# A list scheduler's prices for GpSimd: additions, powers and one-column operations dearer

## The chip, the cores and the metric

The kernel runs on one core of a Trainium2 chip. The metric is the device time of one execution in microseconds. Engines are called as in the profile: PE is TensorE, PEld its weight loads, DVE VectorE, ACT ScalarE, POOL GpSimd, SP SyncE, which issues the transfers.

## The reference, cut to what matters

A decoder trunk of two layers over 1024 tokens of width 1024, everything in float32. Layer 0 mixes by a convolution module, layer 1 by windowed attention on one shared K/V; both have a layer norm behind the mixer, an MLP of width 4096 with a layer norm behind it, and a gated embedding ("ple").

```
for i in range(2):
    if i == 0:
        y = conformer_conv(...)      # w_in, sigmoid gate, 31 taps, layer norm, silu, w_out
    else:
        y = swa_sink_attention(...)  # w_q, rope, window 128, sinks, w_o; K/V from x after layer 0
    x = layer_norm(ALPHA * x + y, mix_g[i], mix_b[i])
    x = layer_norm(ALPHA * x + square(relu(x @ w_up[i])) @ w_down[i], mlp_g[i], mlp_b[i])
    x = x + (p[i] @ w_proj[i]) * sigmoid(x @ w_gate[i])
```

## The kernel before, in words

**The order is planned.** The program does not issue instructions as it goes. `Emit` writes the whole network down as a list of operations (`Recorder.record`), each with its engine, its operands and what it depends on. `Recorder.schedule` then plays that list on a model of the engines and fixes two things for the chip: the order in which each engine takes its instructions, and which buffer of a ring (`SLOTS`: five `t`, sixteen `sm`, six `ps`, two `tr` and so on) a tile gets. In the model an engine takes, of the operations that are ready, the one that was written first; the time after which an operation counts as done is `Recorder.cost`. On the chip the order stays as fixed, but each instruction lasts as long as it lasts, and waits on semaphores for what it needs.

**Operations with a choice.** Additions that are recorded for `either` go in the model to whichever of DVE and GpSimd comes free first. These are the last step of most layer norms (`xt = z * g + b`, the addition) and additions in the embedding stage. `both` and `held` make two-input operations of DVE, and GpSimd's wide ones, exclude each other in the model.

**Precision.** A float32 product is three products of rounded parts: `split` makes a high part `xh` (a rounding copy, "CAST", mostly on ACT) and a low part `xl` (a subtraction on DVE). The same for weights: `raw` arrives by a transfer, ACT makes `wh`, DVE `wl`.

**The places that matter here.** `conv_ln` norms the convolution's output, whose sixteen 128x512 halves lie in the tiles X0 to X7 and A0 to A7. Per 128 tokens: `stats` on DVE, one one-column operation and one power on GpSimd (`sm`, reciprocal root), one one-column operation on DVE (mean times root), then GpSimd scales X and A in place. PE transposes X and A into `tr` or `ps` tiles, ACT applies silu into `t`, and DVE splits `t` into `xh` and `xl`, which frees the `t`. The same `t` ring carries the embedding projections, which ACT copies out of `ps` and SP stores; PE fills its time with those projections while the norm runs. `layer_norm` with `row_stats` closes the mixers and MLPs: three one-column operations and one power on GpSimd per 128 tokens, ACT makes `z`, DVE multiplies, and an `either` adds into `x` (tiles E and B in layer 0, A and B in layer 1). `to_xT` then transposes `x` on PE and splits it.

Of the kernel before, what the change touches and what calls it, by code (L numbers as in the profile page):

```python
# [13 lines left out]
ALU = mybir.AluOpType  # L14
# [185 lines left out]
class Recorder:  # L200
# [90 lines left out]
    def cost(self, o, outs, allv):  # L291
        e, n = o.eng, o.name
        f = outs[0].n if outs and isinstance(outs[0], View) else 1024
        if e == "tensor":
            if n == "transpose":
                return 113.5
            return max(109.0, f * 0.4427 + 5.5 * (f < HT))
        if e == "sync":
            return 380.0
        if e == "scalar":  # L300
            t = 60.0 + f * 0.85
            if n == "activation":
                t += sum(c for k, c in (("bias", 90.0), ("scale", 130.0), ("accum_out", 110.0)) if isinstance(o.kw.get(k), View))
            return t
        if e == "gpsimd":
            if n == "tensor_tensor":
                return 460.0 if o.kw["op"] == ALU.pow else 90.0 + 2.2 * f
            return 160.0 + 1.17 * f
        psum = any(v.buf.space == "PSUM" for v in allv)
        if n == "tensor_scalar" and not psum:  # L310
            return 100.0 + f * 0.69
        if n == "bn_stats":
            return 69.0 + 1.042 * allv[-1].n
        if n == "reduce_max":
            return 70.0 + allv[-1].n * 1.042
        if n == "reciprocal":
            return 60.0 + 6.3 * f
        t = 120.0 if isinstance(o.kw.get("scalar"), View) else 70.0
        return t + f * 1.042
# [1676 lines left out]
```

## Time and profile before

| | |
|---|---|
| median of 3 runs | 2141.74 us (2140.77 to 2145.2) |
| profiled execution, whole | 2140.78 us |
| its span, first to last instruction | 2139.1 us |
| PE busy | 2118.0 us, 99% |
| DVE busy | 1736.6 us, 81% |
| ACT busy | 1144.6 us, 54% |
| GpSimd busy | 285.7 us, 13%, 530 instructions |

PE has work at nearly every moment, so the time is what PE must do and the few microseconds in which it stands still. A table of waits names, for each engine, what ended its idle time. In a timeline a bracket at the end of a row gives the idle time ahead of it and what ended that. All work is recorded through one helper, so all rows carry L469 and are told apart by their tiles.

### The profile page before, as it was taken

Reading aid. Unit: us, or ns where it says so; the run is one execution under the profiler, and the core shown is the slowest. Engines: PE = TensorE matmul, PEld = TensorE weight load, DVE = VectorE, ACT = ScalarE, POOL = GpSimd, SP = SyncE. Lnnn points to the kernel's source line nnn. Section 1 sums busy time; section 2 is a strip of 40 time slices with the busy share of each in tenths; the row PEclk is TensorE's granted clock in tenths of the full one; section 3 lists DMA queues with packets and bytes.
Section 4 is the critical chain, followed back from the end, with each engine's and each line's share of the span. In section 5 each row is a group of like instructions: output and inputs, shape, how many; then the busy total and the mean of one; then the engine's idle time right before and its main releaser. Section 6 shows DMA issues by size and latency. Waiting matters only on the chain.

```text
span 2139.1 us, 29650 instructions
## 1 busy us (share of the span) xinstructions
PE 2118.0 (99%) x9940; PEld 1748.0 (82%) x9940; DVE 1736.6 (81%) x2823; ACT 1144.6 (54%) x2162; POOL 285.7 (13%) x530
## 2 busy tenths in 40 slices
PE   9999999999999999999999999999999999999999
PEld 7888778888888888888788878888888888888877
DVE  6566678898898888876986888689988988788688
ACT  5455673554544633335755888455445554333484
POOL 0000042300000000001310666250000000000042
PEclk9999999999999999999999999999999999999999
DMA  8654664747787856655487022665778785565726
GB/s 256 174 151 142 198 217 159 249 151 257 268 278 266 302 175 208 204 180 211 161 281 252 14 87 80 214 229 190 258 262 294 263 332 173 180 233 170 263 72 233
DMA packets 209928, 443.16 MB, mean 207 GB/s; under 512 B 21744, under 2 KB 57200, under 8 KB 209776
## 3 DMA queue, kind: packets, MB, share of 16 engines
q1 hardware_dynamic: 209776, 441.27, 62.2%
q8 instruction: 78, 1.28, 0.2%
q14 instruction: 74, 0.61, 0.1%
HBM read 296.75 MB, written 144.44 MB: 206 GB/s over the span
## 4 chain that ended last, share of the span: by engine, by line
PE 45%; ACT 2%; DVE 2%; DMA 2%; issue 1%; POOL 0%; SPq 0%; DVEq 0%; ACTq 0%; POOLq 0%
PE ps L469 31%; PE tr L469 14%; ACT z L469 1%; DMA raw<-in_w_kv_dram 0%; ACT wh L469 0%; ACT xh L469 0%; DVE t L469 0%; DMA raw<-form 0%; POOL sm L469 0%; DMA raw<-gate_t 0%; DVE B L469 0%; ACT t L469 0%; DVE z L469 0%; DMA raw<-in_w_q_dram 0%; DMA B<-xsp 0%
## 5 line engine op out<-in xcount | busy, mean ns | idle before, releaser
L469 PE MATMUL ps<-xh 128*128 128x512 f32 x618 | 240.4, 389 | 0.0
L469 PE MATMUL ps<-xl,xh 128*128 128x512 f32 x618 | 240.4, 389 | 0.0
L469 PE MATMUL ps<-xh,xl 128*128 128x512 f32 x618 | 240.4, 389 | 0.0
L469 ACT CAST wh<-raw 128x1024 fp32r<-128x1024 f32 (+2 forms) x158 | 148.2, 941 | 154.9 <-PE ps L469 90.5
L469 PE MATMUL ps<-xl,wh 128*128 128x512 f32 x540 | 210.9, 391 | 0.3 <-DVE xl L469 0.3
L469 PE MATMUL ps<-xh,wl 128*128 128x512 f32 x540 | 210.6, 390 | 0.0
L469 PE MATMUL ps<-xh,wh 128*128 128x512 f32 x540 | 209.3, 392 | 0.4 <-ACT xh L469 0.4
L469 POOL TENSOR_SCALAR sm<-sm 128x1 f32<-128x1 f32 x72 | 25.8, 362 | 1363.7 <-DVE E L469 600.8
L469 PE MATMUL ps<-wh,xh 128*128 128x512 f32 x392 | 154.6, 395 | 2.5 <-DVE t L469 1.5
L469 PE MATMUL ps<-wl,xh 128*128 128x512 f32 x392 | 155.0, 395 | 0.0
L469 PE MATMUL ps<-wh,xl 128*128 128x512 f32 x392 | 154.7, 395 | 0.0
L469 ACT CAST xh<-wh 128x1024 fp32r<-128x1024 f32 x76 | 79.9, 1051 | 116.5 <-PE ps L469 90.3
L469 ACT CAST wh<-g 128x512 fp32r<-128x512 f32 x108 | 65.1, 621 | 140.0 <-DVE g L469 56.2
L469 PEld LDWEIGHTS ps<-xh,xl 128*128 128x128 f32 x618 | 116.0, 188 | 24.3
L469 PEld LDWEIGHTS ps<-xh 128*128 128x128 f32 x618 | 116.0, 188 | 24.0
L469 PEld LDWEIGHTS ps<-xl,xh 128*128 128x128 f32 x618 | 116.0, 188 | 23.9
L469 DVE TENSOR_TENSOR wl<-raw,wh 128x1024 fp32r<-128x1024 f32 (+1 forms) x102 | 103.9, 1020 | 36.1 <-ACT wh L469 34.8
L469 PEld LDWEIGHTS ps<-xh,wh 128*128 128x128 f32 x540 | 101.7, 188 | 22.1 <-ACT xh L469 0.8
L469 PEld LDWEIGHTS ps<-xl,wh 128*128 128x128 f32 x540 | 101.6, 188 | 20.7 <-DVE xl L469 1.4
L469 PEld LDWEIGHTS ps<-xh,wl 128*128 128x128 f32 x540 | 101.4, 188 | 20.6
L469 DVE TENSOR_TENSOR xl<-wh,xh 128x1024 fp32r<-128x1024 f32 x76 | 93.0, 1223 | 24.3 <-ACT xh L469 24.3
L469 DVE TENSOR_TENSOR E<-z,cst 128x832 fp32r<-128x832 f32 x64 | 64.0, 1021 | 57.9 <-PE ps L469 57.9
(425 smaller groups left out, 5642.1 us busy)
## 6 DMA issues: line engine op xcount, KB each, us to landing
wh<-hid SPq DMA_DIRECT2D x78, 512.0 KB, 4.4
raw<-in_w_up_dram SPq DMA_DIRECT2D x61, 512.0 KB, 4.3
wl<-in_w_down_dram SPq DMA_DIRECT2D x58, 512.0 KB, 4.7
hid<-zz SPq DMA_DIRECT2D x96, 256.0 KB, 3.4
hid<-t SPq DMA_DIRECT2D x70, 256.0 KB, 3.0
raw<-hid SPq DMA_DIRECT2D x30, 512.0 KB, 3.8
scr<-zz SPq DMA_DIRECT2D x32, 256.0 KB, 3.7
B<-scr SPq DMA_DIRECT2D x64, 128.0 KB, 4.0
```

The lines of the kernel that those rows point to most:

```text
L469: getattr(getattr(nc, o.eng), o.name)(*a, **k)
```

## The change

Three prices of GpSimd in the model are raised. `f` is the number of columns.

```diff
         if e == "gpsimd":
             if n == "tensor_tensor":
-                return 460.0 if o.kw["op"] == ALU.pow else 90.0 + 2.2 * f
-            return 160.0 + 1.17 * f
+                return 550.0 if o.kw["op"] == ALU.pow else 90.0 + 3.1 * f
+            return (300.0 if n == "tensor_scalar" and f < 8 else 160.0) + 1.17 * f
```

For the shapes that occur: an addition of 512 columns goes from 1216 to 1677 ns, a power from 460 to 550 ns, a one-column operation from 161 to 301 ns. Scalings of 512 columns keep their price of 759 ns. No instruction computes anything else than before. The order on PE is the same up to the convolution's layer norm and differs in places from there on: in the layer norms, the embedding stage of layer 0, the K/V stage and the attention. In the long MLP stages PE's order is the same but for tile numbers. Ten `either` additions move from DVE to GpSimd and nine from GpSimd to DVE.

The first place is the convolution's layer norm. GpSimd before, from the scaling of the tokens of X5 on; `sm12` and `sm6` are the roots for the tokens of X6 and X7:

```order
L469 TENSOR_SCALAR X5_351_619<-X5_351_619,sm13_650_2915 128x512
L469 TENSOR_SCALAR A5_19_83<-A5_19_83,sm13_650_2915 128x512
L469 TENSOR_SCALAR sm12_655_2939<-sm10_652_2928 128x1
L469 TENSOR_SCALAR sm6_659_2957<-sm3_657_2944 128x1
L469 TENSOR_TENSOR sm12_655_2939<-sm12_655_2939,mhalf_242_306 128x1
L469 TENSOR_TENSOR sm6_659_2957<-sm6_659_2957,mhalf_242_306 128x1
L469 TENSOR_SCALAR X6_352_630<-X6_352_630,sm12_655_2939 128x512
```

GpSimd now, at the same place:

```order
L469 TENSOR_TENSOR sm13_650_2915<-sm13_650_2915,mhalf_242_306 128x1
L469 TENSOR_TENSOR sm12_655_2939<-sm12_655_2939,mhalf_242_306 128x1
L469 TENSOR_SCALAR X5_351_619<-X5_351_619,sm13_650_2915 128x512
L469 TENSOR_SCALAR A5_19_83<-A5_19_83,sm13_650_2915 128x512
L469 TENSOR_SCALAR X6_352_630<-X6_352_630,sm12_655_2939 128x512
L469 TENSOR_SCALAR A6_20_84<-A6_20_84,sm12_655_2939 128x512
L469 TENSOR_SCALAR sm6_659_2958<-sm3_658_2947 128x1
L469 TENSOR_TENSOR sm6_659_2958<-sm6_659_2958,mhalf_242_306 128x1
```

The power for `sm12` has moved ahead of X5 and A5, and the one for `sm6` behind X6 and A6. DVE beside it, before (the one-column products with `sm12` and `sm6` stand ahead of the split of the first `t`):

```order
L469 TENSOR_TENSOR wl4_671_3003<-raw1_644_2878,wh3_670_3002 128x1024
L469 SCALAR_TENSOR_TENSOR sm12_655_2939<-sm10_652_2928,sm12_655_2939 128x1
L469 SCALAR_TENSOR_TENSOR sm6_659_2957<-sm3_657_2944,sm6_659_2957 128x1
L469 CAST xh00_243_307<-t1_679_3027 128x2x256
L469 TENSOR_TENSOR xl00_244_308<-t1_679_3027,xh00_243_307 128x2x256
L469 TENSOR_TENSOR wl3_672_3005<-raw0_675_3010,wh4_673_3006 128x1024
L469 TENSOR_TENSOR xl00_244_308<-t2_682_3038,xh00_243_307 128x2x256
```

DVE now:

```order
L469 SCALAR_TENSOR_TENSOR sm12_655_2939<-sm10_652_2928,sm12_655_2939 128x1
L469 TENSOR_TENSOR wl3_671_3002<-raw0_673_3006,wh4_672_3003 128x1024
L469 CAST xh00_243_307<-t1_679_3028 128x2x256
L469 TENSOR_TENSOR xl00_244_308<-t1_679_3028,xh00_243_307 128x2x256
L469 SCALAR_TENSOR_TENSOR sm6_659_2958<-sm3_658_2947,sm6_659_2958 128x1
L469 TENSOR_TENSOR xl00_244_308<-t2_681_3037,xh00_243_307 128x2x256
```

The product with `sm6` now stands between the split of tile t1 and that of tile t2. On ACT, the copies of the projections out of `ps` were, before, the next thing after the first silu half of t4:

```order
L469 CAST xh00_243_307<-t2_682_3038 128x2x256
L469 ACTIVATE t4_690_3077<-tr0_695_3107,cst_240_304 128x256
L469 COPY t1_700_3125<-ps0_680_3030 128x512
L469 ACTIVATE t4_690_3077<-tr0_695_3107,cst_240_304 128x256
L469 COPY t0_693_3088<-ps4_677_3020 128x512
```

ACT now:

```order
L469 ACTIVATE t4_689_3074<-tr0_697_3113,cst_240_304 128x256
L469 ACTIVATE t2_704_3139<-ps1_698_3115,cst_240_304 128x256
L469 ACTIVATE t4_689_3074<-tr0_697_3113,cst_240_304 128x256
L469 ACTIVATE t2_704_3139<-ps1_698_3115,cst_240_304 128x256
L469 CAST xh10_247_311<-t4_689_3074 128x2x256
L469 COPY t0_691_3084<-ps4_676_3018 128x512
L469 COPY t1_701_3131<-ps0_680_3031 128x512
```

The silu into the slot t2, which the split of the old t2 frees, now stands ahead of both copies.

The second place is PE in the last layer norm of the first MLP. Before, the transposes of the tile B3 (the normed tokens 512 to 639) stand here; the products around them are those of the embedding's gate:

```order
L469 MATMUL ps2_1607_9254<-wh0_1538_8811,xh00_243_307 128x512
L469 MATMUL ps2_1607_9254<-wl0_1546_8877,xh00_243_307 128x512
L469 MATMUL ps3_1612_9281<-ident_241_305,B3_961_4546 128x128 x4
L469 MATMUL ps2_1607_9254<-wh0_1538_8811,xl00_244_308 128x512
L469 MATMUL tr1_1615_9298<-wh3_1548_8896,xh10_247_311 128x512
```

Now they stand here:

```order
L469 MATMUL ps2_1615_9317<-wh1_1529_8714,xh00_243_307 128x512
L469 MATMUL ps2_1615_9317<-wl0_1544_8864,xh00_243_307 128x512
L469 MATMUL ps2_1615_9317<-wh1_1529_8714,xl00_244_308 128x512
L469 MATMUL ps4_1613_9301<-ident_241_305,B3_958_4534 128x128 x4
L469 MATMUL ps5_1616_9324<-ident_241_305,B5_1348_6974 128x128 x4
L469 MATMUL ps2_1615_9317<-wh0_1538_8811,xh00_243_307 128x512
```

That is 19 products later than before, counted over PE's whole order. Other transposes move likewise, named by their start in the trace of before: those at 1022.95 us by 11 rows, at 1035.96 us by 10, at 1095.87 us by 8, at 1138.36 us by 10. The product that started at 1045.40 us stands 8 rows earlier. On DVE, the addition that frees the `ps` of the product of 2070.83 us stands 11 rows earlier.

## The prediction

> **What bounds the kernel now.** I read the busy times first, then what each stretch leaves PE idle, then PE's waits.
>
> ```profile
> PE 2118.0 (99%) x9940; PEld 1748.0 (82%) x9940; DVE 1736.6 (81%) x2823; ACT 1144.6 (54%) x2162; POOL 285.7 (13%) x530
> ...
> 250.00:300.00 50.00, 46.23 (x248) 39.17 (x249) 31.34 (x64) 36.60 (x74) 24.52 (x32) 0.97 0.86 274
> 400.00:450.00 50.00, 49.63 (x223) 40.19 (x222) 48.09 (x77) 28.66 (x48) 2.86 (x2) 1.00 0.56 177
> 500.00:1000.00 500.00, 500.00 (x2207) 413.33 (x2206) 418.70 (x586) 228.02 (x333) 0.00 (x0) 1.00 0.72 242
> 1000.00:1050.00 50.00, 47.99 (x240) 38.79 (x239) 42.13 (x77) 40.34 (x79) 23.03 (x37) 1.00 0.15 50
> 1050.00:1100.00 50.00, 49.13 (x228) 40.17 (x227) 45.35 (x71) 32.26 (x52) 10.72 (x3) 1.00 0.79 278
> ```
>
> The first row is the page's; the others are windows (length, then busy time and count of PE, PEld, DVE, ACT, POOL, then PE's clock). PE stands still for 2139.1 - 2118.0 = 21 us of the whole span. From 500 to 1000 us it is never idle, and 500 us over 2207 products gives 0.227 us for each, which I use as the price of a row of PE. There the order can't matter. It can matter where a window has less than its 50 us: 3.8 us missing about the convolution's norm, 2.0 and 0.9 us about the last norm of the first MLP.
>
> ```profile
> PE ps L469 <- ACT t L469: 4.0, 2, 2.7
> PE ps L469 <- DVE t L469: 3.9, 5, 1.5
> PE ps L469 <- DMA B<-scr: 2.6, 2, 1.9
> ...
> PE ps L469 <- ACT zz L469: 0.9, 1, 0.9
> PE ps L469 <- POOL B L469: 0.8, 2, 0.4
> ```
>
> PE's waits (sum, times, longest): the largest, 2.7 us, is one wait for ACT's copies into `t`. GpSimd itself is named with 0.8 us only. It acts through others.
>
> **The prices themselves.** The groups of GpSimd (busy, mean ns | idle):
>
> ```profile
> L469 POOL TENSOR_TENSOR B<-z,g 128x512 f32<-128x512 f32 x16 | 26.1, 1645 | 10.4 <-DVE z L469 7.0 <-PE tr L469 1.7 <-DVE sm L469 1.0
> L469 POOL TENSOR_SCALAR sm<-sm 128x1 f32<-128x1 f32 x72 | 25.8, 362 | 1363.7 <-DVE E L469 600.8 <-DVE A L469 589.0 <-DVE sm L469 156.0
> L469 POOL TENSOR_TENSOR sm<-sm,mhalf 128x1 f32<-128x1 f32 x40 | 24.2, 610 | 2.9
> L469 POOL TENSOR_TENSOR A<-A,t 128x512 f32<-128x512 f32 x3 | 12.3, 4111 | 25.0 <-DVE t L469 19.9 <-PE ps L469 5.1
> L469 POOL TENSOR_TENSOR B<-B,bo 128x512 f32<-128x512 f32 x1 | 1.3, 1297 | 16.6 <-issue 16.6
> ...
> 1064.82 8.84 POOL L469 TENSOR_TENSOR E<-E,t 128x512 f32<-128x512 f32 x1 [18.93 <-DVE t L469]
> ```
>
> The new prices (1677, 550 and 301 ns) are nearer to the means of 1645, 610 and 362 than the old (1216, 460, 161). But the same addition lasts 1.30 us alone and up to 8.84 us beside DVE, so a fixed price is a plan, not a time. No work goes away. What the change is worth is what the new order does to PE's 21 us.
>
> [...]
>
> **Term 1, the convolution's norm.** Timelines of POOL, DVE, ACT and PE:
>
> ```profile
> 280.44 0.78 POOL L469 TENSOR_SCALAR A<-A,sm 128x512 f32<-128x512 f32 x1
> 282.91 1.83 POOL L469 TENSOR_SCALAR X<-X,sm 128x512 f32<-128x512 f32 x1
> 287.10 0.47 POOL L469 TENSOR_SCALAR sm<-sm 128x1 f32<-128x1 f32 x2
> 287.65 1.06 POOL L469 TENSOR_TENSOR sm<-sm,mhalf 128x1 f32<-128x1 f32 x2
> 288.71 1.01 POOL L469 TENSOR_SCALAR X<-X,sm 128x512 f32<-128x512 f32 x1
> ...
> 283.03 1.23 DVE L469 TENSOR_TENSOR wl<-raw,wh 128x1024 fp32r<-128x1024 f32 x1
> 288.75 0.16 DVE L469 SCALAR_TENSOR_TENSOR sm<-sm,sm 128x1 f32<-128x1 f32 x1 [0.36 <-POOL sm L469]
> 289.27 0.98 DVE L469 TENSOR_TENSOR xl<-t,xh 128x512 fp32r<-128x512 f32 x1
> 291.31 0.68 DVE L469 TENSOR_TENSOR xl<-t,xh 128x512 fp32r<-128x512 f32 x1
> ...
> 290.29 0.59 ACT L469 COPY t<-ps 128x512 f32<-128x512 f32 x1 [2.36 <-DVE xl L469]
> 290.77 0.57 ACT L469 ACTIVATE t<-tr,cst 128x256 f32<-128x256 f32 x1
> ...
> 287.16 0.60 PE L469 MATMUL ps<-ident,X 128*128 128x128 f32 x4
> 287.60 0.60 PE L469 MATMUL tr<-ident,X 128*128 128x128 f32 x4
> 290.93 0.50 PE L469 MATMUL ps<-wh,wh 128*128 128x512 f32 x1 [2.73 <-ACT t L469]
> ```
>
> The chain reads backwards: PE waits at 290.93 for ACT's copy of 290.29, which needs a free `t`, which DVE's `xl` of 289.27 frees, which stood behind the product with `sm6` (288.75), which waited for GpSimd's power (done at 287.65 + 1.06 = 288.71).
>
> Now that power stands behind X6 and A6, and the splitting of t2, not t1, is what ACT needs first. GpSimd, from the end of the scaling of A3 (281.22): one one-column operation more ahead, 0.24, and the power for `sm8`, 0.53: 281.99. Two one-column operations, 0.47, X4 and A4, 0.78 each, plus 1.05 for the `wl` that DVE runs beside them (1.83 against 0.78): 285.07. Two powers: 286.13. X5, A5, 1.56, beside the moved `wl` 1.05: 288.74. X6 beside the CAST, 1.01, A6 beside an `xl`, 0.78 + 0.98: 291.5. One-column, 0.24, power, 0.53: 292.3, against 288.71. Then DVE's product, 0.16, and `xl`, 0.68: 293.1. ACT runs four silu halves and casts, about 0.45 apart (0.48 from 290.29 to 290.77), and the copy, 0.59, so that PE goes on at about 295.7, where it was 290.93. It does two groups of transposes more meanwhile, 2 x 0.44 (from 287.16 to 287.60). **+4.8 - 0.9 = +3.9 at most**. Without any collision on GpSimd (0.78 for every scaling) the power ends near 289.1 and the same steps give 292.5 - 290.93 - 0.9 = **+0.7 at least**. A gain would need the power to come earlier, and two more scalings stand ahead of it. I take **+3.4**, near the upper end, since both `wl` rows stand beside those scalings in DVE's order too.
>
> **Term 2, waits that go.** PE's rows with the waits that a later place can hide:
>
> ```profile
> 1022.95 0.63 PE L469 MATMUL ps<-ident,E 128*128 128x128 f32 x4 [0.49 <-DVE E L469]
> 1029.39 0.65 PE L469 MATMUL ps<-ident,B 128*128 128x128 f32 x4 [0.32 <-POOL B L469]
> 1035.96 0.66 PE L469 MATMUL ps<-ident,B 128*128 128x128 f32 x4 [0.43 <-POOL B L469]
> 1045.40 0.50 PE L469 MATMUL ps<-wh,xh 128*128 128x512 f32 x1 [0.76 <-DVE t L469]
> 1095.87 0.66 PE L469 MATMUL ps<-ident,B 128*128 128x128 f32 x4 [0.62 <-DVE xl L469]
> 1138.36 0.41 PE L469 MATMUL ps<-ident,t 128*128 128x128 f32 x2 [0.54 <-DVE B L469]
> 2070.83 0.50 PE L469 MATMUL ps<-wh,xh 128*128 128x512 f32 x1 [0.71 <-DVE t L469]
> ```
>
> The transposes of 1022.95, 1029.39, 1035.96, 1095.87 and 1138.36 move 11, 19, 10, 8 and 10 rows back, at least 1.8 us each, against waits of 0.3 to 0.6: they go, 0.49 + 0.32 + 0.43 + 0.62 + 0.54 = 2.4. The wait at 2070.83 goes too, since the addition that frees its `ps` stands 11 rows earlier on DVE: 0.7. Together **-3.1**; as the same waits can come back at a neighbour, between 0 and -3.1. What is late next: the splits behind those transposes, which the products of the next stage need.
>
> **Term 3, a wait that grows.** The product of 1045.40 comes 8 rows earlier, 1.8 us, for an addition on DVE that keeps its place: between 0 and 1.8 more. DVE's own work ahead of it also depends on PE, so I take half, **+0.9**.
>
> **Term 4, the nineteen additions.** Those that go to GpSimd cost DVE 0.7 us less each, those that come 0.7 to 1.7 more; the balance is one. In the first mixer's norm three come to DVE where it is busy 48.09 of 50 us; two of them late would cost up to 2 us, one early gives nothing. **+0.5**, 0 to 2. The rest lies beside PE's products.
>
> **Term 5, the attention and the other norms.** PE's transposes shift both ways there by up to 19 rows. I take **0**, with -1.5 to +2.
>
> Sum: 3.4 - 3.1 + 0.9 + 0.5 = **+1.7 us**. On the profiled execution, 2140.8 (1.7 around its span), that is 2142.5. The median of the runs, 2141.7, lies 0.9 above it, so the forecast is **2143.4**. The least sum is 0.7 - 3.1 - 1.5 = -3.9, the largest 3.9 + 1.8 + 2 + 2 = 9.7.
>
> **Rivals.** 0.2% is 4.3 us, about what a measurement of this kernel can tell from none.
>
> *Faster.* Later transposes and the truer prices take away most waits everywhere, the one at 290.93 too, because `xl` of t1 comes ahead of `sm6` now and may let PE on. For it: every wait listed is short. Against it: the copies stand behind the silu into t2. It decides if ACT's copy starts before 289.5; then term 1 is -1.5 instead of +3.4, and with terms 3 and 4 at 0 and 5 at -1.5 the sum is -6.1: 2135.6.
>
> *Slower.* One addition on GpSimd beside back-to-back work of DVE holds up a tile that PE transposes for K/V. Four of the ten that move to GpSimd lie between 1060 and 1145 us, where DVE is busy 45.35 of 50 and one addition took 8.84 us. Planned at 1.68, it ends 7.2 late; PE can run some 11 rows, 2.5 us, ahead: +4.7, 2148.1. It decides once an addition there lasts over 4.2 us and its tile is the next one wanted. Against it: the long one of before made PE wait for nothing in that list.
>
> *Nothing.* Waits only change places, and the 2.7 us stays about what it is: 2141.7.
>
> **How the numbers follow.** Forecast 0.43 (of it 0.03 above the upper bound of no change, 2146.0), nothing 0.09, slower 0.28, faster 0.20 (0.01 more from the forecast's lower edge, 2137.5). So slower 0.31, faster 0.21, same 0.48. Alone, the likeliest case spans 2139 to 2147. For 8 in 10 the range takes in the nearer halves of both rivals: 2136 to 2149.
>
> **What would show it.** The window 250 to 300 with PE at 43 instead of 46.23, and one wait of 6 to 7 us for ACT's `t` near 295; the waits on POOL B and DVE E gone; a wait of 1 to 2.5 us on DVE `t` near 1044; GpSimd additions of over 4 us between 1060 and 1145. I am wrong if PE goes on before 293 in the first place, or if the attention between 1150 and 1350 gains or loses over 2 us.

## The result and the profile after

The changed kernel takes 2155.44 us (median of 4 runs, 2152.2 to 2157.16); the kernel before 2142.3 us (4 runs, 2140.77 to 2145.2). The ratio is 1.0062 (95% interval 1.0050 to 1.0074): slower by about 13 us. The forecast was 2143.4 us with a range up to 2149, so the time lies outside it, on the side of the slower rival. The profiled execution is the longest of the four runs (2157.16 us) and the one of before the shortest of its runs (2140.78), so the two traces differ by 16.4 us, 3 us more than the medians.

First the page of the changed kernel, its span and busy times, then windows (length, busy time and count of PE, PEld, DVE, ACT, POOL, PE's granted clock, DMA share, GB/s):

```profile
span 2155.4 us, 29646 instructions
...
PE 2123.4 (99%) x9940; PEld 1750.9 (81%) x9940; DVE 1733.4 (80%) x2822; ACT 1146.4 (53%) x2162; POOL 277.7 (13%) x531
...
250.00:300.00 50.00, 44.45 (x233) 37.18 (x234) 29.70 (x62) 35.00 (x71) 22.32 (x32) 0.93 0.80 264
...
1000.00:1050.00 50.00, 49.39 (x245) 40.70 (x245) 40.44 (x72) 37.35 (x74) 21.21 (x36) 1.00 0.14 41
...
1150.00:1200.00 50.00, 47.28 (x242) 39.07 (x241) 33.42 (x99) 33.79 (x103) 11.59 (x32) 0.97 0.56 193
```

PE now stands still for 2155.4 - 2123.4 = 32.0 us instead of 21, and has 5.4 us more busy time with the same 9940 products: part of them ran at a lower clock (0.93 against 0.97 in the window 250 to 300, 0.97 against 1.00 from 1150 to 1200). The window 250 to 300 lost 1.8 us of PE's work (44.45 against 46.23), 1000 to 1050 gained 1.4, and 1150 to 1200, where PE was busy for 49.52 us before, lacks 2.7.

PE's waits in the changed kernel (sum in us, times, longest):

```profile
PE tr L469 <- ACT t L469: 5.5, 4, 3.2
PE ps L469 <- DVE xl L469: 3.0, 2, 2.2
...
PE ps L469 <- DMA wl<-gate_low_t: 2.2, 1, 2.2
```

The waits on POOL `B` and DVE `E` of before are gone, as the prediction said. Waits of over 2 us are four now, 3.2, 2.5, 2.2 and 2.2, where before had one.

To see where the time went, take the two traces and the start of the same row of PE by count (row 1376, row 1700 and so on). PE has the same number of rows in both, so the time between two such rows can be compared though the order within differs (only at row 5420 do five of the rows ahead of it differ too):

| PE's stage | before, us | after, us | difference |
|---|---|---|---|
| up to the convolution's norm | 272.4 | 270.5 | -1.9 |
| convolution's norm | 69.3 | 74.2 | +4.9 |
| first mixer's output and norm | 130.8 | 132.2 | +1.4 |
| first MLP | 535.3 | 536.1 | +0.8 |
| last norm of the first MLP | 43.5 | 41.8 | -1.7 |
| embedding of layer 0 | 50.8 | 52.5 | +1.7 |
| K/V, entry into the attention | 67.3 | 70.5 | +3.2 |
| attention, second mixer | 371.7 | 373.1 | +1.4 |
| second MLP and its norm | 546.4 | 546.9 | +0.5 |
| end | 45.6 | 51.5 | +5.9 |

The order on PE ahead of the convolution's norm is the same in both; the -1.9 there is a stretch of half clock at 252 us that the trace of before has and this one hasn't (0.50 against 1.00 from 252 to 255). Two things follow for the reading. Times of the two traces can't be set side by side as they stand: the changed kernel reaches row 1376, the start of the convolution's norm, at 272.05 us, the kernel before at 273.95, so 1.9 us have to be added to a time of the changed kernel near 290 to put it on the clock of before. And each line of the table is one execution of each kernel; how far the same order can differ from one execution to the next is told in the last section.

**The convolution's norm.** POOL, DVE, ACT and PE in the changed kernel, then two windows:

```profile
284.80 1.99 POOL L469 TENSOR_SCALAR A<-A,sm 128x512 f32<-128x512 f32 x1
...
289.07 0.55 POOL L469 TENSOR_TENSOR sm<-sm,mhalf 128x1 f32<-128x1 f32 x1
...
289.65 0.16 DVE L469 SCALAR_TENSOR_TENSOR sm<-sm,sm 128x1 f32<-128x1 f32 x1 [2.33 <-POOL sm L469]
289.73 0.69 DVE L469 TENSOR_TENSOR xl<-t,xh 128x512 fp32r<-128x512 f32 x1
...
290.51 0.56 ACT L469 ACTIVATE t<-ps,cst 128x256 f32<-128x256 f32 x1 [2.40 <-DVE xl L469]
...
285.82 0.66 PE L469 MATMUL tr<-ident,A 128*128 128x128 f32 x4 [0.90 <-ACT t L469]
287.71 0.66 PE L469 MATMUL tr<-ident,X 128*128 128x128 f32 x4 [0.76 <-ACT t L469]
291.58 1.11 PE L469 MATMUL tr<-ident,A 128*128 128x128 f32 x4 [3.22 <-ACT t L469]
...
290.00:297.00 7.00, 5.42 (x18) 4.59 (x19) 5.12 (x9) 5.79 (x12) 2.49 (x2) 0.52 0.32 98
```

The chain is the forecast one: PE waits for ACT's silu, ACT for a free `t2`, that for DVE's split of 289.73, which stands behind the product with `sm6`, which waits for GpSimd's power. The power ends at 289.07 + 0.55 = 289.62, on the clock of before 291.5, which is 2.8 us later than its 288.71. The kernel z_conv below, which has the same order here and starts the stage within 0.13 us of before, says the same without a correction, 291.15 + 0.55 = 291.70:

```profile
291.15 0.55 POOL L473 TENSOR_TENSOR sm<-sm,mhalf 128x1 f32<-128x1 f32 x1
```

There are three waits in the changed kernel, each ahead of a group of transposes, 0.90 + 0.76 + 3.22 = 4.9 us, instead of the one of 2.73: 2.2 more. Behind them PE is granted half its clock for about 7 us: 5.42 us of work at 0.52 could have been done in 2.8, another 2.6 lost. 2.2 + 2.6 = 4.8, against 4.9 in the table.

**The end.** One row of PE's waits, POOL and SP before:

```profile
PE tr L469 <- DMA wl<-gate_low_t: 0.3, 1, 0.3
...
2097.12 9.44 POOL L469 TENSOR_TENSOR A<-A,t 128x512 f32<-128x512 f32 x1 [19.15 <-DVE t L469]
...
2106.59 0.34 SPq L469 DMA_DIRECT2D out_dram<-A  x1
2107.97 0.32 SPq L469 DMA_DIRECT2D wl<-gate_low_t  x1
```

and in the changed kernel, with one row of DVE, PE and windows:

```profile
2109.12 11.85 POOL L469 TENSOR_TENSOR A<-A,t 128x512 f32<-128x512 f32 x1 [24.14 <-DVE t L469]
...
2119.71 0.70 DVE L469 TENSOR_TENSOR zz<-zz,tr 128x512 f32<-128x512 f32 x1
...
2120.99 0.34 SPq L469 DMA_DIRECT2D out_dram<-A  x1
2121.39 0.42 SPq L469 DMA_DIRECT2D wl<-gate_low_t  x1
...
2122.35 0.47 PE L469 MATMUL ps<-wh,xh 128*128 128x512 f32 x1 [1.30 <-DVE zz L469]
2126.40 0.80 PE L469 MATMUL ps<-wl,xh 128*128 128x512 f32 x1 [2.20 <-DMA wl<-gate_low_t]
...
2095.00:2125.00 30.00, 27.48 (x118) 21.51 (x116) 30.00 (x51) 18.36 (x28) 12.71 (x2) 1.00 0.53 181
2126.00:2130.00 4.00, 3.60 (x9) 2.88 (x10) 0.38 (x1) 0.59 (x1) 1.55 (x2) 0.57 1.02 384
```

One addition on GpSimd, beside a DVE that is never idle (30.00 of 30 us), takes 11.85 us, where its new price is 1.68. It ends 1.26 us after the start of DVE's row at 2119.71, the first in that time that takes one of its inputs from a `tr` or `ps` tile; the last section comes back to this. The store of its tile waits for it on SP, and the load of the weight `wl` stands behind that store; PE then waits 2.20 us for `wl`. Before, the same addition took 9.44 us and the same store stood ahead of the same load, but PE waited only 0.3 us for it. Counted from row 9730, where the end begins, the addition was over after 17.6 us then and is after 21.5 now, and the load went out after 19.0 and 21.9. So the store's place is not new; before, the addition was simply over in time. After the waits PE is again at about half clock (0.57): 3.60 us of work there cost some 1.5 more than at full clock.

**The entry into the attention.** PE and a window in the changed kernel:

```profile
1165.60 0.47 PE L469 MATMUL ps<-wh,xh 128*128 128x512 f32 x1 [2.46 <-ACT B L469]
...
1167.00:1170.00 3.00, 3.00 (x8) 2.19 (x8) 1.97 (x9) 1.56 (x4) 0.00 (x0) 0.51 0.92 300
```

A product waits 2.46 us, and half clock follows here too: 3 us of work at 0.51, and with 1170 to 1171, which has 0.75, some 3.4 us at half clock in all. The longest wait of that stretch before:

```profile
1162.48 0.41 PE L469 MATMUL ps<-ident,t 128*128 128x128 f32 x2 [0.47 <-ACT X L469]
```

### The profile page after: what moved, and what is told of

Same layout as the page of the kernel before. It is cut to its first block, busy times and chain, and to the rows that moved or that the text cites. A ratio compares the mean times of both kernels' runs of the same rounds, so it can differ in the third digit from the quotient of the medians.

```text
span 2155.4 us, 29646 instructions
## 1 busy us (share of the span) xinstructions
PE 2123.4 (99%) x9940; PEld 1750.9 (81%) x9940; DVE 1733.4 (80%) x2822; ACT 1146.4 (53%) x2162; POOL 277.7 (13%) x531
## 3 DMA queue, kind: packets, MB, share of 16 engines
q8 instruction: 78, 1.28, 0.2%
## 4 chain that ended last, share of the span: by engine, by line
PE 77%; DVE 4%; ACT 3%; DMA 2%; POOL 1%; issue 1%; SPq 0%; DVEq 0%; ACTq 0%; POOLq 0%
PE ps L469 58%; PE tr L469 19%; ACT z L469 1%; DVE xl L469 1%; POOL A L469 1%; DMA raw<-gate_t 1%; ACT wh L469 1%; DMA t<-proj 1%; ACT t L469 1%; DVE z L469 0%; DVE sm L469 0%; DVE X L469 0%; DMA xh<-in_w_gate_dram 0%; ACT xh L469 0%; DVE t L469 0%
## 5 line engine op out<-in xcount | busy, mean ns | idle before, releaser
L469 PE MATMUL ps<-xh 128*128 128x512 f32 x636 | 247.4, 389 | 0.0
L469 PE MATMUL ps<-xl,wh 128*128 128x512 f32 x584 | 228.1, 391 | 0.0
L469 PE MATMUL ps<-xh,wl 128*128 128x512 f32 x584 | 227.3, 390 | 0.0
L469 PE MATMUL ps<-xh,wh 128*128 128x512 f32 x584 | 226.2, 391 | 0.4 <-ACT xh L469 0.4
L469 PE MATMUL ps<-wh,xh 128*128 128x512 f32 (+1 forms) x388 | 155.0, 400 | 7.6 <-ACT B L469 2.5
L469 PE MATMUL ps<-wl,xh 128*128 128x512 f32 (+1 forms) x388 | 154.9, 399 | 2.2 <-DMA wl<-gate_low_t 2.2
L469 PE MATMUL ps<-wh,xl 128*128 128x512 f32 (+1 forms) x388 | 154.4, 398 | 0.0
L469 PEld LDWEIGHTS ps<-xh,wh 128*128 128x128 f32 x584 | 109.9, 188 | 24.7 <-ACT xh L469 0.8
L469 PEld LDWEIGHTS ps<-xh,wl 128*128 128x128 f32 x584 | 109.7, 188 | 22.4
L469 PEld LDWEIGHTS ps<-xl,wh 128*128 128x128 f32 x584 | 109.9, 188 | 21.3 <-DVE xl L469 0.6
```

Of the source, the lines that this page charges most:

```text
L469: getattr(getattr(nc, o.eng), o.name)(*a, **k)
```

## Experiments: which place loses how much

The schedule is one greedy pass, so a price that holds only for the operations of one stage (they are numbered in program order) gives the changed order there and leaves the old one nearly everywhere else.

```diff
         if e == "gpsimd":
+            if o.num < 3200:                 # z_conv
+            if 3200 <= o.num < 5000:         # z_mix0, instead
+            if 5000 <= o.num < 13500:        # z_mid, instead
+            if 18000 <= o.num:               # z_end, instead
+                ...the three new prices...
             if n == "tensor_tensor":
                 return 460.0 if o.kw["op"] == ALU.pow else 90.0 + 2.2 * f
             return 160.0 + 1.17 * f
```

> The new prices hold only for the operations up to the convolution's layer norm; the order there is the changed kernel's, row by row, and from the first MLP on the old kernel's. Theory A (each place loses by itself what its own waits and its own slow clock show): +4.4 us on the old kernel, 2146 to 2147, PE's three waits for ACT's t near 286, 288 and 291 us of 0.9, 0.8 and 3.2 us, and some 6 us at a granted clock of 0.5 behind 290. Theory B (the loss is a matter of the whole, as of drifting transfers, and one place alone loses little): within 1.5 us of the old kernel.

> The new prices hold only for the operations of the first mixer's output and its layer norm. Theory A: the waits of 1.5 us for DVE's wl at 400 and 0.7 and 0.2 us for ACT's t behind it come back, +2.1 us, and perhaps +0.8 at 612: 2144 to 2145. Theory B: within 1 us of the old kernel.

> The new prices hold only from the last layer norm of the first MLP through the embedding stage, K/V and the attention. Theory A: -1.7 us in the norm, +1.4 in the embedding, +3.8 at the entry into the attention (a wait of 2.5 us for ACT near 1158 and 3.4 us of half clock behind it): +3.5, 2145 to 2146. Theory B: within 1.5 us of the old kernel.

> The new prices hold only from the last layer norm of the second MLP to the end. Theory A: GpSimd's last long addition again takes about 12 us, PE again waits 1.3 us for DVE's zz and 2.2 us for the load of wl near 2110, with 3.4 us of half clock behind: +5.5, 2147 to 2148. Theory B: within 1.5 us of the old kernel.

The kernel before took 2140.92 us beside these four. z_conv: 2145.55, ratio 1.0022 (1.0013 to 1.0031). z_mix0: 2144.59, 1.0021 (1.0012 to 1.0030). z_mid: 2144.27, 1.0016 (1.0007 to 1.0025). z_end: 2147.15, 1.0030 (1.0019 to 1.0042). Each part alone is slower; together they make 0.89%, more than the whole's 0.62% (0.50 to 0.74). They share one reference, so their errors add up together and the sum is loose. The second mixer's norm, in which three of the nineteen additions change engine, is in none of the four.

In its own trace z_mix0 loses only 1.1 us in its own stage. Most of the rest, 3.8 us in the first MLP, is a wait near 610 us, in a stage whose order on PE is that of before, and half clock behind it:

```profile
610.02 0.74 PE L473 MATMUL tr<-X,wh 128*128 128x512 f32 x2 [1.97 <-ACT t L473]
...
604.00:620.00 16.00, 14.03 (x55) 11.09 (x54) 12.22 (x21) 5.63 (x11) 0.00 (x0) 0.89 0.76 261
```

That wait is 0 in before and in z_conv, 0.62 in the changed kernel, 1.39 in z_mid, with the same rows around it: it comes and goes. What it follows from was not found, so z_mix0's time, in the range of theory A, is in part luck.

## Experiments: the convolution's norm

> The kernel with the new prices for the convolution's norm alone (z_conv), and in it one row moved by hand: DVE's split of t2 stands ahead of the product with sm6, which waits for GpSimd's power. Theory A (that one product, queued in front of the split, holds ACT and so PE): ACT's wait of 2.4 us for DVE's xl goes, PE's wait of 3.2 us near 291 falls under 1.2, the clock stays at 1.0 there; 2145.5 falls to 2141 to 2142. Rival (GpSimd's late scalings of X5 to X7 hold PE's next transposes in any case): the wait only changes its name and the time stays within 1 us of z_conv.

```diff
-            for o in self.schedule():
+            order = self.schedule()          # prices as in z_conv
+            ahead(2805, 3029)                # DVE: split xl of t2 ahead of the product with sm6
+            for o in order:
```

2142.27 us against 2141.75, ratio 1.0002 (0.9993 to 1.0011): the loss of z_conv is gone from the time, by one row of DVE. PE and a window in it:

```profile
288.91 0.66 PE L492 MATMUL tr<-ident,A 128*128 128x128 f32 x4 [0.89 <-ACT t L492]
290.36 0.50 PE L492 MATMUL ps<-wh,wh 128*128 128x512 f32 x1 [0.34 <-ACT t L492]
...
290.00:296.00 6.00, 4.89 (x25) 3.85 (x25) 5.27 (x9) 5.00 (x10) 2.83 (x2) 1.00 0.46 154
```

The last wait is 0.89 + 0.34 us instead of 3.26 in z_conv, and without a long wait the clock stays at 1.00 in this trace. The shorter waits ahead of it are still there, and a new one of 0.77 us for GpSimd's scaling of A, so the rival is right in a small part: all of PE's waiting in this stage falls from 4.9 to 3.5 us only. The stage takes 71.0 us against z_conv's 74.2, and more than half of the 3.2 between them is the half clock that no longer follows. GpSimd's power is no earlier than in z_conv (it ends at 289.96, and this trace is 2.2 us ahead of z_conv's); what counted was that a split which needs nothing from it stood behind it in DVE's queue.

The same holds in the kernel before, whose 2.73 us wait has this cause too. There the splits of both tiles were moved ahead of the products with `sm12` and `sm6`, with the old prices:

```diff
+            # DVE: cast and split of t1, split of t2, ahead of the product with sm12
+            order = self.merge(self.schedule(), ((2794, 3018), (2795, 3018), (2805, 3018)))
```

> The kernel before, with its own order but for three rows of DVE in the convolution's norm: the rounding of t1 and the splits of t1 and t2 stand ahead of the two products with sm12 and sm6 that wait for GpSimd. Theory A: the wait of 2.7 us, PE's longest, shrinks to under 1 us: 2138 to 2139.5, faster than both kernels. Rival (X6 and X7 are scaled later instead and PE waits for them): within 1 us of the kernel before.

2139.53 us against 2141.75, ratio 0.9990 (0.9981 to 0.9999): a little faster than the kernel before, just clear of the noise. The wait falls to

```profile
289.85 0.50 PE L516 MATMUL ps<-wh,wh 128*128 128x512 f32 x1 [0.79 <-ACT t L516]
```

## Experiments: the end

> The kernel with the new prices for the end alone (z_end), and in it SP's store of the tile that GpSimd adds to for 12 us moved behind the three loads of weights that stood behind it. Theory A (the store waits for the addition and holds the loads in SP's queue): the load of wl is issued some 2 us earlier, PE's wait of 2.2 us for it goes and the 3 to 6 us of half clock behind it with it; 2147.2 falls to 2142.5 to 2144, leaving the waits near 2075 and 2111. Rival (the buffer of wl comes free late, or the transfers themselves are slow): within 1 us of z_end.

```diff
+            behind(19573, 19750)             # SP: store of A behind the three loads; prices as in z_end
```

2143.03 us against 2141.75, ratio 1.0008 (0.9999 to 1.0017), where z_end had 1.0030.

```profile
2097.28 11.85 POOL L492 TENSOR_TENSOR A<-A,t 128x512 f32<-128x512 f32 x1 [24.00 <-DVE t L492]
...
2107.65 0.32 SPq L492 DMA_DIRECT2D wl<-gate_low_t  x1
2109.87 0.42 SPq L492 DMA_DIRECT2D out_dram<-A  x1
```

The addition is as long as in z_end, and PE no longer waits for `wl`, for which it waited 2.72 us there, with a granted clock of 0.66 over the 10 us from 2114 on: the late addition cost time through the store that stands ahead of the loads in SP's queue, not by its length alone.

> As z_end, with the long addition itself done by DVE instead of GpSimd, at its place in the order. Theory A: 0.7 us on DVE instead of 12 on GpSimd, the store and the loads behind it go out early: 2142.5 to 2144.5, some 0.5 more than with the store moved, since DVE has no idle time there. Rival (DVE is what bounds this stretch): as z_end or up to 1 us more.

```diff
+            ops[19572].eng = "vector"        # the long addition on DVE; prices as in z_end
```

2144.74 us, ratio 1.0013 (1.0005 to 1.0022). Taking the long addition away from GpSimd also recovers more than half. Where the rest lies its trace does not settle: PE waits 1.18 us for ACT's `wh` at the end, but that stage is 1.0 us shorter than in s_end_sp, and the stage ahead of it is 1.1 us longer, since here half clock follows a wait of 2.19 us that both kernels have there (the products behind it start 0.43 us apart, in s_end_sp 0.23). The two repairs can't be told apart by their times.

## Experiments: the entry into the attention

Three tries, each on top of the one before it, with the prices of z_mid.

> As z_mid (new prices from the last norm of the first MLP through the attention), with five rows of the K/V stage moved by hand: ACT's two copies of the third tile of keys and values stand ahead of a weight's rounding, and DVE's three products that release that tile's ps stand ahead of the K splits, as in the kernel before. Theory A (the queues of ACT and DVE hold the last reader of the ps that PE wants): PE's wait of 2.5 us at the entry into the attention and the 3.4 us of half clock behind it go; +3.4 on the kernel before falls to 0 or below, 2140.5 to 2142, since the norm ahead of it is 1.7 us shorter. Rival (transfers of w_q are late there): as z_mid.

> The middle part's new order (operations 5000 to 13499) with six rows restored: the five of the run before (ACT's two copies of one K/V tile ahead of a weight rounding, DVE's three zz additions of that tile ahead of the first K addition) and, new, DVE's addition t<-zz of the same tile ahead of the two K additions too. Theory, the transposes waited 2.11 us for t because that addition stood behind two K additions and the split of X on DVE, which in turn waited for ACT's K copies: it can now run near 1154.9 instead of 1157.77, PE's wait at the transposes goes, and the stretch at the entry of the attention falls from 22.4 us to 19.6 to 20.5; the time to 1.0002 of the kernel before (0.9993 to 1.0010), from 1.0014. Rival, the wait moves on again, to the next tile's transposes or to the products behind them: the stretch stays at 22 us and the ratio at 1.0010 to 1.0018.

> The middle part's new order with thirteen rows of the attention's entry restored: the six of the run before, three DVE rows of the last K/V tile (zz, zz, t) ahead of the split of X, and on PE the two pairs of transposes of the last two K/V tiles, each four products later, as in the kernel before. Theory, the entry loses because PE's new order asks for these transposes two and eight products behind the ones before them, where it was six and ten, while the chain ACT's copies, DVE's zz additions, t for one tile takes as long as before; each repair on one engine alone therefore only moved the wait. With both, PE's wait of 2.42 us goes: the entry takes 19.6 to 20.4 us, not 22.6, and the time is 1.0000 to 1.0006 of the kernel before. Rival, another wait takes its place again (the products behind the transposes, for a ps): the entry stays over 21.5 us, the ratio at 1.0010 to 1.0016.

```diff
+            # s_att, one K/V tile. ACT: two copies ahead of a rounding; DVE: three zz additions
+            # ahead of the first K addition
+            (10497, 10555), (10500, 10555), (10501, 10471), (10502, 10471), (10503, 10471)
+            # s_att2, further. DVE: t<-zz of that tile ahead of the first K addition
+            (10504, 10471)
+            # s_att3, further. DVE: zz, zz, t of the last tile; PE: two pairs of transposes
+            # four products later
+            (10521, 10132), (10522, 10132), (10523, 10132)
+            (10506, 10588), (10507, 10588), (10525, 10598), (10526, 10598)
```

| kernel | ratio to before (95%) | entry (rows 5330 to 5420), us |
|---|---|---|
| before | | 19.6 |
| z_mid | 1.0016 (1.0007 to 1.0025) | 22.8 |
| s_att | 1.0014 (1.0005 to 1.0022) | 22.4 |
| s_att2 | 1.0013 (1.0004 to 1.0022) | 22.6 |
| s_att3 | 1.0014 (1.0005 to 1.0023) | 23.5 |

All three are misses. The one long wait of PE in each trace, z_mid first, then s_att, s_att2, s_att3:

```profile
1159.51 0.47 PE L473 MATMUL tr<-wh,xh 128*128 128x512 f32 x1 [2.47 <-ACT B L473]
...
1158.05 0.44 PE L520 MATMUL ps<-ident,t 128*128 128x128 f32 x2 [2.11 <-DVE t L520]
...
1161.98 0.41 PE L520 MATMUL ps<-ident,t 128*128 128x128 f32 x2 [2.42 <-DVE t L520]
...
1171.54 1.12 PE L520 MATMUL ps<-ident,t 128*128 128x128 f32 x4 [2.65 <-POOL t L520]
```

Each repair takes away the wait that it aimed at, and one of the same size appears at the next group of transposes: the next K/V tile, then the q tiles. PE's new order asks for each of these groups four or more products earlier than before, and the chain ACT, DVE or GpSimd, DVE that feeds them is not faster. That fits all four traces, but no run took the loss away, so the cause of these 3 us stays open between PE's order and that of the engines which feed it. About 1 us of it is the clock: half clock follows the wait in all four (0.79 over the 8 us about it), while in three kernels below a wait of 2.1 to 2.7 us at this place is followed by none (the clock is 1.00), and there the entry takes 21.6 (s_best), 21.6 (a_two) and 22.0 us (a_four).

A kernel with s_att's five rows and b_conv's three:

> s_att and the three rows of DVE of b_conv in the convolution's norm together. Theory A, with places that add up: b_conv's -2.2 and s_att's: 2138 to 2140, faster than the kernel before and than b_conv by up to 1.7. Rival (no gain from the norm of the first MLP outlasts the next stages): as b_conv.

2141.48 us against 2142.39, ratio 0.9998 (0.9989 to 1.0007). Not better than b_conv alone: in its trace the last norm is 1.7 us shorter than before, and the K/V stage with the entry 2.0 longer.

## Experiments: which price, and the whole change repaired

> Only the prices of the power and of the one-column operation are raised, that of the addition is the old one. The order in the convolution's norm is the changed kernel's, that of K/V and attention the old one. Theory A (each place pays for its own order): +4.5 from the convolution's norm, nothing from the attention, the end unknown: 2145 to 2150. Rival (the dearer additions are what costs): within 2 us of the kernel before.

> Only the price of the addition is raised. The order in the convolution's norm is the old one; the mixers' norms, the norm of the first MLP, K/V, attention and the end are new. Theory A: none of the 4.5 us of the convolution's norm, some of the 13 others: 2143 to 2150. Rival (the two small prices alone cost it): within 2 us of the kernel before.

```diff
-                return 460.0 if o.kw["op"] == ALU.pow else 90.0 + 2.2 * f
-            return 160.0 + 1.17 * f
+                # p_small: powers 550, additions as before, one-column operations 300
+                # p_add: powers as before, additions 90.0 + 3.1 * f, one-column as before
```

p_small: 2147.8 us against 2142.39, 1.0026 (1.0015 to 1.0037); its convolution's norm takes 73.3 us of PE (69.3 before), and its second MLP with the norm behind 550.2 (546.4). p_add: 2147.24, 1.0028 (1.0016 to 1.0039); its convolution's norm has the order of before, but near the end PE waits 4.95 us at a product where the changed kernel waits 2.19 and the kernel before not at all:

```profile
2077.62 0.80 PE L469 MATMUL ps<-wh,xh 128*128 128x512 f32 x1 [4.95 <-DVE xl L469]
```

Both times lie in the ranges of theory A and outside those of the rivals. So no single price is to blame: each set of prices gives another order, with losses in places of its own.

> The whole changed kernel with two repairs: on DVE the split of the tile t2 ahead of the product with sm6 in the convolution's norm, and on SP the last store of a tile A behind the three loads that it held up. Theory, these two places made the same loss in the whole change as each did alone (0.20% and 0.22%): 1.0062 - 0.0020 - 0.0022 = 1.0020 of the kernel before, about 2146 us. Rival, the losses don't add (the four parts alone sum to 0.89% where the whole is 0.62%), so the two repairs bring only seven tenths of their 0.42%: 1.0033, about 2149.

> The whole changed kernel with the two repairs and the six restored rows at the entry of the attention. If the six rows take away that wait in the middle part alone, 0.12% less than with two repairs: 1.0008 of the kernel before, about 2143.5 us, and the entry takes 19.6 to 20.5 us of PE instead of 22.8. If the wait moves on, the time is that of the two repairs.

> The whole changed kernel with the two repairs (the split of t2, SP's store) and the thirteen rows of the attention's entry. Theory: 2.0 to 3 us less than with the two repairs alone, 1.0034 of the kernel before, about 2149 less whatever the run-to-run wait near 606 us does; the entry takes 19.6 to 20.4 us. Rival, the wait moves: as with the two repairs, 1.0046, and the entry at 21.5 us or more.

```diff
+            # the three new prices everywhere. a_two: split of t2; three loads ahead of the store
+            order = self.merge(self.schedule(), ((2805, 3029), (19744, 19573), (19830, 19573), (19750, 19573)))
+            # a_three: and the six rows of s_att2; a_four: and the thirteen of s_att3
```

a_two: 2150.33 us against 2141.69, 1.0046 (1.0033 to 1.0060). a_three: 2150.3, 1.0038 (1.0026 to 1.0051). a_four: 2150.86 against 2141.58, 1.0050 (1.0036 to 1.0064). The two repairs bring 13.1 - 8.6 = 4.5 us by the medians and 0.16% by the ratios, where the parts alone promised 0.42%; with intervals of 0.12 and 0.13% to either side that gain is itself hardly clear of the noise. The simple sum (1.0020) is not borne out, and the rival (1.0033) is only at the edge of the interval. The traces say more for the repairs: in a_two the convolution's norm takes 71.0 us instead of 74.2, the end 47.0 instead of 51.5, 7.7 together, and no half clock follows in either place; but that profile is the shortest of its runs and the one of the changed kernel its longest. What a_two still loses against before is spread by its trace: 1.7 in the convolution's norm, 1.6 in the first mixer, 1.1 in the first MLP, 1.1 in the embedding, 2.0 at the entry, 1.4 at the end, less 1.7 in the last norm. Rows at the entry change nothing here either.

## Why the prediction was wrong

- **Term 1, +3.4.** Size nearly right: +4.9 in the trace, 4.6 timed alone (2145.55 - 2140.92), above the upper end of 3.9. The chain was right, and s_conv shows it: one DVE row in it removes the loss. The working was close too, once the 1.9 us are added by which this trace is ahead: the power ends at 291.5 against the 292.3 worked out, and the product that PE ran at 290.93 starts at 293.20, on the clock of before 295.1, against 295.7. So the sign "PE goes on before 293" is not met, though the transposes at 291.58 seem to meet it. What the sum left out is the half clock, 2.6 of the 4.9 us; the waiting alone adds 2.2, in three waits and not in one of 6 to 7 us. That the total came near 3.4 is in part luck.
- **Term 2, -3.1.** The three waits of the last norm went, and its stage is 1.7 us shorter. The others were replaced. 1095.87 and 1138.36 came back as 0.81 and 0.25, and a new one of 1.15 us on ACT's `wh` came in the embedding stage, which is 1.7 us longer. At 2070.83 the wait went, and so did one of 0.93 us at 2084.75 that was not counted, but one of 2.19 us came, for a split: the "late next" of the prediction, three times as large as the 0.71 gained. These and the rows of the next two points:

```profile
399.99 1.42 PE L469 MATMUL ps<-wh,wl 128*128 128x512 f32 x5 [1.47 <-DVE wl L469]
1047.81 0.50 PE L469 MATMUL ps<-wh,xh 128*128 128x512 f32 x1 [0.48 <-DVE t L469]
1084.24 0.47 PE L469 MATMUL ps<-wh,xh 128*128 128x512 f32 x1 [1.15 <-ACT wh L469]
1103.01 0.66 PE L469 MATMUL ps<-ident,B 128*128 128x128 f32 x4 [0.81 <-DVE xl L469]
2086.19 0.50 PE L469 MATMUL ps<-wh,xh 128*128 128x512 f32 x1 [2.19 <-DVE xl L469]
```

  By these waits term 2 was in fact near 0, the upper end of what was given: the gains were counted, and the waits behind them were only named.
- **Term 3, +0.9.** Wrong sign: that product (now at 1047.81, above) waits 0.48 us for DVE's `t`, where it was 0.76.
- **Term 4, +0.5.** The first mixer lost 1.4, 1.1 alone in z_mix0: within the 0 to 2 given. The wait is for a split weight (1.47 us for DVE's `wl` at 399.99, above), not for the result of an addition. One of the three additions that came to DVE does stand ahead of that `wl` (0.68 us at 392.20), but DVE also stood idle between them, so what the addition had to do with it stays open.
- **Term 5, 0, from -1.5 to +2.** Mis-sized: the entry lost 3.2 and the attention with the second mixer 1.4. The prediction's own test, over 2 us lost between 1150 and 1350, is met.
- **The missing term.** "The rest lies beside PE's products" is the step that failed most: the end, +5.9 us, was not worked out at all. z_end (0.30%) and s_end_sp (0.08%) show that most of it comes from the addition that ends late, through the store ahead of the loads in SP's queue.
- **The slower rival** had the right mechanism, an addition on GpSimd of over 4.2 us beside back-to-back DVE, at the wrong place and by the wrong way. Between 1060 and 1145 no addition took over 2.26 us; the one of 11.85 stands at the end, and what it held up was not a tile for a transpose but a store, and with it a load. The quoted addition of 8.84 us made the prediction look at the middle; the one of 9.44 us, at the end, was in the trace of before as well, so "up to 8.84 us" was not the longest either.

The new prices are nearer to the means, as the prediction said. The group from which the addition's price can be read now has this mean:

```profile
L469 POOL TENSOR_TENSOR B<-z,g 128x512 f32<-128x512 f32 x14 | 23.3, 1676 | 9.8 <-DVE z L469 7.4 <-ACT z L469 1.0 <-PE ps L469 0.8
```

The price 1677 meets the mean of that group, 1676, though its single additions take 1.28 to 2.29 us, and it is a seventh of the 11.85 us where it mattered.

## What to carry to other kernels

A truer price in a greedy planner is not a truer plan: where PE is 99% busy the old order has little left to gain, and every order that new prices gave here brought new waits whose size no mean duration tells. When an order changes, follow each queue through the places where the old order was tight, SP's queue too, and look for a row that needs nothing from the row it stands behind: moving that one row (a split behind a product, a load behind a store) was worth more than the prices. Do not count a wait as gained before what comes next on the same chain has been sized.

## What the runs showed of the hardware

Three of PE's waits in the changed kernel cost more than their length. Behind those of 3.22, 2.46 and 2.20 us the granted clock was 0.51 to 0.57. Products of 512 columns at 294 us start 0.43 us apart, and again 0.23 at 298:

```profile
293.77 0.63 PE L469 MATMUL ps<-wl,wh 128*128 128x512 f32 x1
294.20 0.63 PE L469 MATMUL ps<-wh,wl 128*128 128x512 f32 x1
...
298.30 0.39 PE L469 MATMUL ps<-wh,wl 128*128 128x512 f32 x1
298.53 0.39 PE L469 MATMUL ps<-wh,xh 128*128 128x512 f32 x1
```

It isn't a matter of the wait's length alone. The same wait of 2.73 us at the same rows had no half clock behind it in the kernel before and had it in z_mix0, and the one of 2.19 us at 2086 in the changed kernel had none, where in s_end_dve half clock follows a wait of 2.19 us for the same product. The window 290 to 296 of before, of z_mix0, and 2080 to 2100 of the changed kernel:

```profile
290.00:296.00 6.00, 5.07 (x26) 4.23 (x27) 5.96 (x8) 5.71 (x12) 6.00 (x3) 1.00 0.61 176
...
290.00:296.00 6.00, 6.00 (x26) 4.89 (x25) 5.17 (x7) 4.69 (x10) 4.24 (x3) 0.72 0.88 193
...
2080.00:2100.00 20.00, 17.82 (x87) 14.54 (x86) 14.64 (x22) 12.98 (x22) 4.80 (x5) 1.00 0.87 303
```

The old order of the convolution's norm was traced ten times, each time with one wait of 2.5 to 2.7 us for the same product. In before, z_end and s_end_sp the clock stayed at 1.00 behind it, and the stage took 69.3 us; in z_mix0, z_mid, s_end_dve, p_add and the three tries at the entry it was 0.79 over 288 to 296, and the stage took 70.8 or 70.9. So 1.5 of the 4.9 us in the table hang on which execution of the kernel before was profiled.

What decides whether half clock follows a wait was not shown. The loss of 2.6, 1.5 and 1.5 us behind three such waits, 5.6 us in all, is a price that the prediction left out; against it stands the one stretch of half clock at 252 us in the trace of before, the -1.9 of the table.

The other number is the 11.85 us of one 512-column addition on GpSimd beside a DVE without idle time, the same to 0.01 us in the changed kernel, z_end and s_end_sp, where the shortest addition of the changed kernel takes 1.28. It is not a random length. In the traces of before, the changed kernel, z_mid, z_end, s_end_sp, p_add, a_two and a_three eleven additions on GpSimd took more than 2.7 us, from 8.84 to 11.86. Each of them ends 1.23 to 1.26 us after the start of DVE's first row that takes an input from a `ps` or `tr` tile; all rows of DVE up to there take both inputs from other tiles (1.25 us for both of before, 1.26 for the one of the changed kernel). So the end of such an addition followed the end of DVE's run of these rows, and one price for all additions can't hold that; why it did was not shown. The 1.30 us that the prediction calls alone were not alone: at 1091.44 in the trace of before DVE was busy for 1.20 of them, and two of its rows there took an input from a `ps` tile.
